# First FFN of a hybrid decoder layer: where a pair's products for the 16 learned tokens stand among the products of its up quad

## The chip, the cores and the metric

One core of a Trainium2 chip runs the whole layer. The metric is the time of one execution on the device, in microseconds (us). The engines of the core work side by side, each through its own queue in order: TensorE (PE in the profile, its weight loads PEld) multiplies matrices into PSUM banks, VectorE (DVE) and ScalarE (ACT) work element by element, GpSimd (POOL) mostly issues stores, SyncE (SP) issues most loads. They meet at semaphores.

## What is computed

16 learned ("meta") tokens stand ahead of 1024 tokens of 1024 values each, 1040 in all. The layer is a half-step gated FFN, a projection with two kinds of heads, an output projection and a second half-step FFN, each on normed tokens:

```python
def swiglu(h, w_in, w_out):
    gu = h @ w_in
    g, u = jnp.split(gu, 2, axis=-1)
    return (jax.nn.silu(g) * u) @ w_out

h = h + 0.5 * swiglu(rms_norm(h, ffn1_norm[l]), ffn1_w_in[l], ffn1_w_out[l])
```

All in float32. The case is about the first line of `swiglu` in the first FFN: 1024 input values, 2 x 2816 columns (gate g and up u), for the 1024 tokens and for the 16 learned ones.

## The kernel before

**Tiles.** `fast_in` (from L351) makes the first FFN's `h @ w_in` for the 1024 tokens. It takes 256 columns of gate and the same 256 of up at a time, a *pair*; there are 11 pairs. The gate half and the up half of a pair are each a *quad*: a 2 x 2 block product (two halves of the 1024 inputs, two blocks of 128 columns, two halves of 512 tokens) done with seven block products instead of eight (Winograd's scheme). The token side has seven ready operands, named B11, T2, B21, T3, T1, T4, B22 in the order in which a quad uses them; the weight side has seven to match: a11, s2, a12, s3, s1, a22, s4.

**Weights of a quad.** `block` (L367) loads four blocks of 128 x 512 float32 (256 KB each) from SP into buffers of tag raw, of which there are 10; the order is a11, a21, a22, a12. DVE makes the sums s1 = a21 + a22, s2 = s1 - a11, s3 = a11 - a21, s4 = a12 - s2 (L382, tag s, three buffers). `operand` (L358) splits each of the seven into a rounded part (ACT, L360) and a rest (DVE, L362), three buffers each, so that the split of an operand starts when the product three places ahead of it has ended. A product is 12 matmuls of 128 x 512 (L450).

**What happens to a product.** B11 and B21 go to bank qa, T2, T3 and T4 to qb, T1 and B22 to qc; a bank that takes several products in turn is read between them. After B11 ACT copies qa (p1). After T2 DVE reads qb (u2, L482), after T3 again (u3). After T1 DVE reads qc (L533 in a gate quad, u at L543 in an up quad), then after T4 qb, then after B22 qc. So T3 may not start before u2 has read qb, nor B22 before u has read qc; one other product stands between each time. In a gate quad ACT takes silu of the results; in an up quad DVE multiplies by them, and POOL stores.

**Learned tokens.** Their products can't use the block scheme; `begin` (L988), which `fast_in` calls as `meta(col, blocks)`, makes them from the same raw blocks. When it is called for a gate quad, it only keeps the four blocks, so their buffers stay in use. When it is called for the up quad, it first calls `finish` for the pair before (a transpose mf on PE at L978, silu sgm on ACT at L981, actm on DVE at L982), then issues 64 small matmuls (mq, L1001) that read all eight raw blocks of the pair, those of the first input half first, and a copy mt on ACT (L1010). sgm, mt and actm are placed after the last instruction of ACT and of DVE that belongs to a main product ("marks").

**Order.** PE's order is the order of the program text (`manual_schedule` for PE). The order of DVE, ACT, SP and POOL is laid out when the kernel is built, by a planner with a model of times: of what it takes to be ready, the earliest in the program's text first. The first eight quads (four pairs, "opened") run interleaved, in turns; the other seven pairs run one quad after the other (L609 to L612). Between the main work, single steps of other work are put in: splitting later weights ahead of time (L180, L181, stores L175), and transposing tokens (L1046).

**After it.** `fast_out` (L615) multiplies by `w_out` (L732, bank o). Its first buffers for `w_out` blocks (L634) and activations (L639) lie where B11 and B21, the first operands to be read for the last time, lay before.

The generator that hands out a quad's weight operands, one for each `next`, is this:

```python
            if not opened:
                yield operand(a11)
...
            yield operand(s3 if sums else made(a11, on.tensor_sub, a21, turns))
            if meta:
                meta(col, [(q, b) for q, b in zip(quarters, blocks)])
            yield operand(s1)
```

What stands between two `yield`s is issued when the next operand is asked for, which `go` (L459) does right ahead of its matmuls. So the learned tokens' group stands on PE between the quad's fourth product (T3) and its fifth (T1).

Of the kernel before, what the change touches and what calls it, by code (L numbers as in the profile page):

```python
# [48 lines left out]
class Block:  # L49
# [300 lines left out]
    def fast_in(self, ops, n, w_in, actD, openers, ev0, open_ev, feed=None, meta=None, spare=None,  # L350
# [7 lines left out]
        def operand(src):  # L358
            hi = wp.tile([P, 4, P], F32R, tag="wh", name="wh", bufs=3)
            nc.scalar.copy(hi, src)  # L360
            lo = wp.tile([P, 4, P], F32R, tag="wl", name="wl", bufs=3)
            self.block_lo = nc.vector.tensor_sub(lo, src, hi.bitcast(F32))  # L362
            return hi, lo
# [3 lines left out]
        def block(i, h, col):  # L367
            t = wp.tile([P, 4, P], F32, tag="raw", name="raw", bufs=self.in_bufs)
            with self.tc.issue_after(loaded[-1].ins) if loaded else ExitStack():
                loaded.append(nc.sync.dma_start(  # L370
                    t, w_in[512 * h : 512 * h + 512, col + P * i : col + P * i + P]
                    .rearrange("(k p) f -> p k f", p=P)
                ))
            self.block_load = loaded[-1]
            return t

        def made(x, op, y, turns):
            if turns == 2:
                t = self.early_raw.tile([P, 4, P], F32, tag="raw", name="s", bufs=4)
            else:  # L380
                t = wp.tile([P, 4, P], F32, tag="s", name="s", bufs=3)
            taken(op(t, x, y), False)  # L382
            return t
# [3 lines left out]
        def parted(src):  # L387
            places[0] += 1
            tags = ("wh", "wl") if places[0] % 2 else ("raw", "raw")
            got = []  # L390
            for i, tag in enumerate(tags):
                t = wp.tile([P, 4, P], F32R, tag=tag, name="w" + "hl"[i],
                            bufs=self.in_bufs if tag == "raw" else 3)
                nc.sync.dma_start(t.bitcast(F32).rearrange("p k f -> p (k f)"), src[:, i])
                got.append(t)
            return got

        prepared = {}
        quarters = (0, 0), (1, 0), (1, 1), (0, 1)
# [3 lines left out]
        def first_sums(blocks, turns, on):  # L403
            a11, a21, a22, _ = blocks
            s1 = made(a21, on.tensor_add, a22, turns)
            return s1, made(s1, on.tensor_sub, a11, turns)
# [11 lines left out]
        def weights(col, opened, turns):  # L418
            if opened and feed:
                for i, src in enumerate(self.parted2[col]):  # L420
                    first = self.first_w.pop(0) if self.first_w and i == 0 else None
                    yield first or parted(src)
                return
            if opened:
                for h in range(2):
                    yield operand(block(0, h, col))
            blocks, sums = prepared.pop(col, (None, None))
            blocks = blocks or [block(i, h, col) for i, h in quarters]
            a11, a21, a22, a12 = blocks
            if not opened:  # L430
                yield operand(a11)
            if sums:
                s1, s2, s3, s4 = sums
            else:
                s1, s2 = first_sums(blocks, turns, on)
            yield operand(s2)
            if not opened:
                yield operand(a12)
            yield operand(s3 if sums else made(a11, on.tensor_sub, a21, turns))
            if meta:  # L440
                meta(col, [(q, b) for q, b in zip(quarters, blocks)])
            yield operand(s1)
            yield operand(a22)
            yield operand(s4 if sums else made(a12, on.tensor_sub, s2, turns))
# [9 lines left out]

        def quad(col, take, opened=None, turns=0, keep=None):
            w = weights(col, opened, turns)
            ps, ready = {}, []

# [133 lines left out]
        opened = [q for f in range(0, 2 * openers, 2) for q in pair(f, "first")]  # L592
# [1799 lines left out]
```

## Time and profile before

| | us |
|---|---|
| median of 3 runs | 1959.63 (1957.4 to 1960.16) |
| profiled execution | 1959.65 |
| its span in the trace | 1957.9 |
| first and last start of an mq matmul | 79.2 and 461.1 |
| mt copies on ACT (L1010): count, median of one | 11, 0.266 |

The span is the time from the first to the last instruction that the profile holds; the execution's own time has 1.7 us around it. All times "at" something are counted from the start of the span. PE's granted clock was 1.00 in every stretch that is shown. A row of a view of stretches has, after start:end, the length, the busy time of PE, PEld, DVE, ACT and POOL, each with its count of instructions, then the granted clock, the share that the DMA engines were busy, and GB/s. A row of a wait view has who waited, for whom, the total in us, how many times, and the longest. A row of a timeline has start, duration, engine, line, operation, tiles, and in brackets the idle time ahead of it with what ended it.

### The profile page before, as it was taken

How to read it: one execution, taken by the hardware profiler on the slowest of the kernel's cores; microseconds unless marked ns; L12 is line 12 of the kernel's file. 1: busy time of each engine (PE TensorE's matmuls, PEld its weight loads, DVE VectorE, ACT ScalarE, POOL GpSimd, SP SyncE). 2: the span in 40 equal slices, each digit the busy share in tenths (PEclk: the TensorE clock that was granted, in tenths of full speed). 3: DMA queues.
4: the chain of work that ended last, by engine and by line, in shares of the span. 5: the costliest groups of instructions: out<-in, count | busy, mean ns of one | idle time of the engine just before them, and what ended most of it. 6: DMA issues, size and time to landing. Idle time of an engine off the chain costs nothing.

```text
span 1957.9 us, 30218 instructions
## 1 busy us (share of the span) xinstructions
PE 1919.8 (98%) x10607; PEld 1616.6 (83%) x10607; DVE 1390.4 (71%) x2184; ACT 849.6 (43%) x1711; POOL 450.5 (23%) x625
## 2 busy tenths in 40 slices
PE   7999999999999999999999999999999999999999
PEld 6888888788888888888898978887888888888887
DVE  7977877877678665467777766677567767766774
ACT  6523443334444544356666635433232332344443
POOL 3010100001000003133333332210544645530000
PEclk9999999999999999999999999999999999999999
DMA  7356887758965315865454177655634444469473
GB/s 213 93 165 170 253 272 243 233 203 291 375 221 188 127 54 144 193 170 148 128 148 121 57 253 225 161 208 183 198 115 140 128 131 121 132 243 318 154 231 113
DMA packets 381687, 355.54 MB, mean 182 GB/s; under 512 B 129040, under 2 KB 284560, under 8 KB 381536
## 3 DMA queue, kind: packets, MB, share of 16 engines
q1 hardware_dynamic: 359728, 288.98, 48.7%
q0 software_dynamic: 20768, 64.63, 9.5%
q8 instruction: 84, 1.38, 0.3%
q14 instruction: 67, 0.55, 0.1%
q10 hardware_dynamic: 1040, 0.00, 0.0%
HBM read 237.95 MB, written 115.57 MB: 181 GB/s over the span
## 4 chain that ended last, share of the span: by engine, by line
PE 89%; DVE 4%; DMA 3%; ACT 2%; issue 1%; POOL 1%; SPq 1%; DVEq 0%; ACTq 0%; POOLq 0%
PE o L732 21%; PE qb L450 18%; PE qa L450 12%; PE qc L450 12%; PE proj L249 5%; PE proj L251 4%; PE proj L250 4%; PE flip L1495 2%; PE wo L250 1%; PE wo L249 1%; PE wo L251 1%; PE mq L1001 1%; PE oacc L1572 1%; PE oacc L1570 1%; DMA oT<-oD 1%
## 5 line engine op out<-in xcount | busy, mean ns | idle before, releaser
L450 PE MATMUL qb<-T,wh 128*128 128x512 f32 x1056 | 344.6, 390 | 1.3 <-ACT T L309 0.8
L450 PEld LDWEIGHTS qb<-T,wh 128*128 128x128 f32 x1056 | 198.1, 188 | 46.4 <-issue 2.5
L450 PE MATMUL qa<-B,wh 128*128 128x512 f32 x696 | 226.7, 390 | 0.3 <-ACT B L835 0.2
L249 PE MATMUL proj<-xh,wh 128*128 128x512 f32 (+2 forms) x640 | 213.2, 333 | 2.6 <-ACT st L1142 1.3
L732 PE MATMUL o<-t,w 128*128 128x512 f32 x924 | 211.8, 390 | 0.7 <-DVE u L543 0.7
L251 PE MATMUL proj<-xl,wh 128*128 128x512 f32 (+2 forms) x640 | 210.2, 328 | 0.8 <-DVE xl L1957 0.8
L250 PE MATMUL proj<-xh,wl 128*128 128x512 f32 (+2 forms) x640 | 210.1, 328 | 0.0
L732 PE MATMUL o<-parts 128*128 128x512 f32 x924 | 209.6, 389 | 0.0
L450 PE MATMUL qb<-T,wl 128*128 128x512 f32 x528 | 205.5, 389 | 0.0
L732 PEld LDWEIGHTS o<-t,w 128*128 128x128 f32 x924 | 172.8, 188 | 37.8 <-ACT sgm L981 1.1
L732 PEld LDWEIGHTS o<-parts 128*128 128x128 f32 x924 | 173.5, 188 | 36.0
L362 DVE TENSOR_TENSOR wl<-s,wh 128x512 fp32r<-128x512 f32 x160 | 165.6, 1035 | 50.8 <-ACT wh L360 49.9
L360 ACT CAST wh<-s 128x512 fp32r<-128x512 f32 x160 | 99.2, 622 | 188.5 <-PE qb L450 141.1
L450 PEld LDWEIGHTS qa<-B,wh 128*128 128x128 f32 x696 | 130.5, 188 | 28.0 <-DVE B L836 0.5
L360 ACT CAST wh<-raw 128x512 fp32r<-128x512 f32 x120 | 74.4, 621 | 155.8 <-PE qc L450 111.4
L450 PE MATMUL qa<-B,wl 128*128 128x512 f32 x348 | 135.4, 389 | 0.0
L249 PEld LDWEIGHTS proj<-xh,wh 128*128 128x128 f32 x640 | 120.8, 189 | 15.0 <-ACT st L1142 2.2
L251 PEld LDWEIGHTS proj<-xl,wh 128*128 128x128 f32 x640 | 120.7, 189 | 12.3 <-DVE xl L1957 1.2
L250 PEld LDWEIGHTS proj<-xh,wl 128*128 128x128 f32 x640 | 120.8, 189 | 10.1
L450 PE MATMUL qc<-B,wh 128*128 128x512 f32 x352 | 115.1, 390 | 2.3 <-DVE u L543 2.3
L450 PE MATMUL qc<-T,wh 128*128 128x512 f32 x352 | 117.0, 394 | 0.0
L450 PEld LDWEIGHTS qb<-T,wl 128*128 128x128 f32 x528 | 99.1, 188 | 20.2
(393 smaller groups left out, 3819.4 us busy)
## 6 DMA issues: line engine op xcount, KB each, us to landing
raw<-in_ffn_w_in_dram SPq DMA_DIRECT2D x176, 256.0 KB, 4.0
raw<-in_ffn_w_out_dram SPq DMA_DIRECT2D x112, 256.0 KB, 4.5
w2in<-both SPq DMA_DIRECT2D x28, 512.0 KB, 3.4
raw<-in_w_in_dram SPq DMA_DIRECT2D x25, 512.0 KB, 5.2
ks<-kD SPq DMA_DIRECT2D x32, 260.0 KB, 4.8
wout<-both SPq DMA_DIRECT2D x16, 512.0 KB, 3.7
wh<-w2in SPq DMA_DIRECT2D x27, 256.0 KB, 3.1
wl<-w2in SPq DMA_DIRECT2D x27, 256.0 KB, 3.1
```

The costliest lines, as they stand in the source:

```text
L249: nc.tensor.matmul(ps, wh[:, s], xs, start=k == 0, stop=False)
L250: nc.tensor.matmul(ps, wl[:, s], xs, start=False, stop=False)
L251: nc.tensor.matmul(ps, wh[:, s], xl[:, k, c0 : c0 + n], start=False, stop=k == nk - 1)
L360: nc.scalar.copy(hi, src)
L362: self.block_lo = nc.vector.tensor_sub(lo, src, hi.bitcast(F32))
L450: nc.tensor.matmul(ps, a[:, k, :], b[:, k, :], start=start and k == 0 and i == 0, stop=k == 3 and i == 2, skip_group_check=True,)
L732: nc.tensor.matmul(banks[bank][m], y[:, m * P : (m + 1) * P], z, start=start and at == 0 and e == 0, stop=q == nq - 1 and e == 2, skip_gro ...
L1001: nc.tensor.matmul(ps[at : at + 32, :], self.xm[:, 4 * h + k, :], got[i, h][:, k, :], start=h == 0 and k == 0, stop=h == 1 and k == 3, til ...
L1495: self.nc.tensor.transpose(ps[:m, j, :], src[:, s0 : s0 + m], self.ident)
L1570: nc.tensor.matmul(o[:, c], vj, w[0], start=j == 0, stop=False, skip_group_check=True)
L1572: nc.tensor.matmul(o[:64, c], vj[:, :64], w[1], start=False, stop=end, skip_group_check=True)
```

## The change

In a quad of one of the seven pairs that are not opened, `meta` is now called ahead of the first operand, right after the four blocks' loads are issued; in an opened pair it stays where it was. For a gate quad the call only keeps the blocks. For an up quad the group (mf of the pair before, mq, and the work on ACT and DVE that hangs on them) now stands on PE ahead of the quad's first product, B11, instead of between T3 and T1.

```diff
             a11, a21, a22, a12 = blocks
+            if meta and not opened:
+                meta(col, [(q, b) for q, b in zip(quarters, blocks)])
             if not opened:
                 yield operand(a11)
             if sums:
...
             yield operand(s3 if sums else made(a11, on.tensor_sub, a21, turns))
-            if meta:
+            if meta and opened:
                 meta(col, [(q, b) for q, b in zip(quarters, blocks)])
             yield operand(s1)
```

The second FFN calls `fast_in` without `meta`; nothing changes there.

## The prediction

> **What bounds the kernel now.** I read the engine table first, then the busy time of the first FFN in stretches cut at the start of each pair's T1 product, and then the waits of TensorE (PE) in these stretches.
>
> ```profile
> PE 1919.8 (98%) x10607; PEld 1616.6 (83%) x10607; DVE 1390.4 (71%) x2184; ACT 849.6 (43%) x1711; POOL 450.5 (23%) x625
> ...
> 256.66:297.01 40.35, 40.35 (x234) 33.28 (x234) 31.63 (x51) 16.60 (x30) 3.79 (x7) 1.00 0.91 279
> 297.01:337.35 40.34, 40.34 (x235) 33.22 (x234) 32.60 (x53) 15.93 (x29) 3.80 (x7) 1.00 0.77 241
> 337.35:379.40 42.05, 40.58 (x234) 33.21 (x234) 32.61 (x53) 16.04 (x29) 3.79 (x7) 1.00 0.69 222
> 379.40:420.40 41.00, 40.69 (x234) 33.27 (x235) 32.02 (x52) 15.83 (x29) 3.79 (x7) 1.00 0.61 209
> 420.40:461.35 40.95, 40.48 (x234) 33.09 (x234) 32.02 (x52) 16.04 (x29) 3.79 (x7) 1.00 0.63 220
> ...
> PE qc L450 <- DVE u L543: 2.3, 3, 1.5
> ```
>
> PE is busy 98% of the span, so the change can win only what PE idles in this stage. A pair without a stall takes 40.35 us. The three stretches from 337.35 on take 42.05, 41.00 and 40.95: 1.70 + 0.65 + 0.60 = **2.95 us** too much. The wait row names 2.3 of it: three times the B22 product (bank qc) waits until DVE has read that bank (u, L543).
>
> Why DVE is late there is in the chain that ended last, first a pair with a stall, then the loads of the next two, then a pair without one (start, duration, what).
>
> ```profile
> 335.34 0.11 PE mf L978
> 335.45 1.02 PE mq L1001 x32
> 336.47 5.15 DMA raw<-in_ffn_w_in_dram
> ...
> 341.71 0.70 DVE s L382
> 342.42 0.02 issue
> 342.44 1.29 DVE s L382 x2
> 343.73 0.61 DVE u L543
> 344.35 0.14 issue
> 344.48 1.63 PE qc L450 x6
> ...
> 378.52 3.98 DMA raw<-in_ffn_w_in_dram
> ...
> 419.43 4.21 DMA raw<-in_ffn_w_in_dram
> ...
> 254.77 1.88 PE mq L1001 x64
> 256.66 2.95 PE qc L450 x12
> 259.61 2.49 PE qb L450 x11
> ...
> 284.13 2.72 PE qa L450 x12
> ```
>
> Half of the learned tokens' group (mq, 32 of 64 matmuls, 1.02 us) has to pass before blocks of this pair's gate are free. Only then SP loads the next gate's remaining blocks there (5.15 us). DVE, which works in order, stands at the sum a21 + a22 of that next gate (L382) until a22 lands, and behind it waits u, for which PE waits. The DVE's waits say how regular this is (six pairs from 216.35 on), and its timeline gives two of the waits that did not reach PE:
>
> ```profile
> DVE s L382 <- DMA raw<-in_ffn_w_in_dram: 22.7, 6, 4.8
> ...
> 300.27 0.69 DVE L382 TENSOR_TENSOR s<-raw 128x512 f32<-128x512 f32 x1 [3.73 <-DMA raw<-in_ffn_w_in_dram]
> ...
> 341.71 0.69 DVE L382 TENSOR_TENSOR s<-raw 128x512 f32<-128x512 f32 x1 [4.83 <-DMA raw<-in_ffn_w_in_dram]
> ```
>
> DVE stands still in every pair; PE feels it only where load and sums together outlast PE's work up to B22.
>
> **The change part by part.** *What moves.* In the 7 pairs after the four opened ones, mf (0.11 us), mq (1.88) and what hangs on them (ACT's sgm and mt copy, DVE's actm) go from between T3 and T1 to ahead of B11, four products of 2.72 = 10.9 us earlier. No instruction is added or removed, so PE's work stays: 0. The product after the group takes 2.95 instead of 2.72; that 0.23 passes from T1 to B11: 0.
>
> *The wait removed.* Count from the start of mq. Before: 1.88 + 2.95 + 2.72 (T1, T4), so B22 could start at 7.55; in the pair above the bank was free at 344.48 − 335.45 = 9.03, 1.48 late. Afterwards the first product to need a bank that DVE has just read is the up quad's T3 (it adds to T2's bank, which u2 reads first). It comes after B11 (2.95), T2 and B21 (2.72 each): 1.88 + 8.39 = 10.27. Even if the whole old chain, load, three sums and a read of the bank, stood ahead of it, it would be through at 9.03, **1.24 us to spare**, and this was the worst of the pairs. It should not even stand there:
>
> ```profile
> 246.50 2.72 PE qb L450 x12
> ...
> 248.19 0.69 DVE L362 TENSOR_TENSOR wl<-s,wh 128x512 fp32r<-128x512 f32 x1 [1.10 <-ACT wh L360]
> 248.92 0.69 DVE L382 TENSOR_TENSOR s<-raw,s 128x512 f32<-128x512 f32 x1
> ```
>
> The sums of a quad have three buffers (tag s), and the up quad's fourth sum (248.92) takes the one that s3's split (248.19) leaves. The next gate's first sum finds a buffer only after that. The fourth sum comes 248.92 − 246.50 = 2.42 after T2's start; with T2 at 1.88 + 2.95 = 4.83 from mq, that is 7.25, later than the load's 1.02 + 5.15 = 6.17. So the block should be there before DVE asks, and of the 22.7 us little should be left. What is late next is nothing: around T1 to B22 only the usual splits remain. I take the full −2.95; bounds 0 (the wait moves along) and −2.95.
>
> The Trainium skill, "DMA: Bandwidth & Descriptors", "Anatomy of one DMA", prices a transfer at about 2.0 us plus bytes over 436 KB/us (fitted on another issue path), which would be an estimate of 2.6 us for these 256 KB. The rows say 3.98 to 5.15. By the page's price old B22 would never have waited for a load and the change would bring 0.
>
> *The wait added.* PE now needs all eight blocks of the pair before B11, and everything on PE queues behind mq.
>
> ```profile
> 255.79 4.01 SPq L370 DMA_DIRECT2D raw<-in_ffn_w_in_dram  x6
> ...
> DMA to landing us min/median/max: 4.0/4.8/7.0
> ```
>
> Six loads, the up quad's four last among them, are out by 259.80 and down by 266.8 even at the longest 7.0; that up quad begins at 284.13. 17 us of cover, and earlier release only widens it: 0. If it went, each us late would be a us of PE, seven times.
>
> *Slack that shrinks.* T1, T4 and B22 lose the 2 us that the group gave their operands. Those are split three products ahead, as buffers come free; 0, bounds 0 to +0.5. On ACT, mt and sgm now stand behind the gate's last silu; ACT is 43% busy and nobody waits for them before the next pair: 0.
>
> *The end of the stage.* In the last pair the token operands B11 and B21 are read for the last time, and so freed, 1.99 us later against the end of the stage (1.88 + 0.11), and w_out's first loads go to that place.
>
> ```profile
> 452.16 0.38 SPq L634 DMA_DIRECT2D raw<-in_ffn_w_out_dram  x1
> 456.44 0.32 SPq L639 DMA_DIRECT2D act<-act10B  x1
> 456.80 0.43 SPq L634 DMA_DIRECT2D raw<-in_ffn_w_out_dram  x1
> 458.94 0.32 SPq L175 DMA_DIRECT2D w2in<-both  x1
> 459.36 0.40 SPq L639 DMA_DIRECT2D act<-act11B  x1
> 459.82 0.90 SPq L634 DMA_DIRECT2D raw<-in_ffn_w_out_dram  x1
> ...
> PE o L732 <- DVE u L543: 0.7, 1, 0.7
> ```
>
> The first load and the 456.44/456.80 pair move by 2; the third load, whose split stands in DVE's queue ahead of the last u, goes back to back behind them and moves from 459.82 to about 460.3. So the 0.7 us that PE waits there grows by about 0.4. Bounds: −0.7 and +2.0. I take +0.4, nearest to the SP rows.
>
> **Sum:** −2.95 + 0.4 = −2.55. The profiled execution took 1959.65 us (span 1957.9 and 1.7 around it), the median of the runs is 1959.63: 1959.65 − 2.55 = **1957.1 us**.
>
> **The rivals.**
>
> *A. The wait moves along.* The planner puts DVE's and SP's queues in order; it can put the next gate's loads behind a store that waits on SP, or its sum elsewhere ahead of a bank read, and DVE stalls as before. For: its order already trusted loads that came 3.7 to 4.8 us late. Against: the buffer count and 1.24 us of spare. 1959.6 us; chance 0.13.
>
> *B. Slower: DVE blocks the up quad's T3.* The same DVE wait, now ahead of u2 in all seven pairs. It decides at 10.27 us after mq's start. With the longest landing, 1.02 + 7.0, three sums (2.02), u2 (0.61) and issue (0.14) make 10.79: 0.52 late, and with one more split of 0.60 queued between, 1.12. Seven times 1.12 is 7.8; less the 2.95 saved, +4.9: 1964.5 us. Over 0.98 per pair the kernel is slower by over 0.2%. Against: the median landing is 4.8. Chance 0.12.
> The Trainium skill ("DMA: Bandwidth & Descriptors", "Latency and other measured facts") lets HBM access grow from 0.2 us to 2 us under load, so loads moved into a fuller stretch would land up to 1.8 us later, an estimate: 9.03 + 1.8 = 10.83, this rival without the extra split (1960.6). The trace does not bear it out: DVE waited 3.73 us at a DMA share of 0.91 and 4.83 at 0.69.
>
> *C. The end of the stage takes it back.* The ring's 2 us go fully to PE: 1959.65 − 2.95 + 2.0 = 1958.7; chance 0.13. Against: the third load's place above.
>
> *D. Faster: the new order helps later stages.* Only PE's order is written out by hand; the rest is planned anew behind the change.
>
> ```profile
> PE flip L1495 <- DVE wu L1619: 3.6, 9, 0.8
> ...
> PE z L1640 <- ACT sig L1643: 1.9, 5, 0.5
> PE flip L1495 <- DVE wm L1619: 1.8, 3, 0.6
> ```
>
> Of these 7.3 us, half gone would give 1953.5. It can as well add; nothing in the rows says which. Chance 0.14.
>
> **How the numbers follow.** Forecast 0.48. A measurement of this kernel tells about 0.2% (3.9 us) from no change, so faster means under 1955.7 and slower over 1963.5. Forecast, A and C lie within: 0.74, of which 0.02 goes to faster for a forecast that also loses the 0.7 at the stage's end and a little more. Faster 0.16, same 0.72, slower 0.12. The range 1954.5 to 1961.5 leaves out B at its price and half of D, about 0.19; it holds A, C and B's small form.
>
> **What would show it.** Right: pair stretches of 40.35 us throughout; no PE wait for u at qc; DVE's 22.7 us at L382 nearly gone; SP rows of the next gate's loads about 11 us earlier against B22; the mt copy right behind a silu. Wrong: a PE wait at qb (T3) for u2, or at mq for a DMA; more than 1.2 us at the first o product; PE waits of the later stages that differ by more than 1 us in sum.

## The result, and the profile after

| | median, us (lowest to highest) | runs | ratio to before (95% interval) |
|---|---|---|---|
| before | 1959.13 (1956.74 to 1962.09) | 21 | |
| changed | 1961.88 (1960.06 to 1964.73) | 21 | 1.0014 (1.0008 to 1.0020) |

The change makes the kernel 2.75 us **slower**, where 2.55 us faster was forecast. The time lies just above the range's end of 1961.5.

The stage that the change was about did what was forecast. This is the view of stretches of the changed kernel, cut again at the start of each pair's T1 (length, busy PE, PEld, DVE, ACT, POOL, granted clock, DMA share, GB/s):

```profile
256.76:297.06 40.30, 40.30 (x234) 33.28 (x234) 32.25 (x51) 16.24 (x30) 3.77 (x7) 1.00 0.90 281
297.06:337.37 40.31, 40.31 (x235) 33.29 (x234) 33.07 (x53) 15.81 (x29) 3.80 (x8) 1.00 0.79 247
337.37:377.68 40.31, 40.31 (x235) 33.29 (x234) 33.06 (x53) 15.81 (x29) 3.78 (x7) 1.00 0.75 238
377.68:417.99 40.31, 40.31 (x234) 33.29 (x234) 32.45 (x52) 15.81 (x29) 3.78 (x7) 1.00 0.61 205
417.99:458.30 40.31, 40.31 (x234) 33.29 (x234) 31.23 (x50) 15.81 (x29) 3.78 (x7) 1.00 0.50 184
```

Every pair takes 40.31 us and PE is never idle: the 42.05, 41.00 and 40.95 are gone. DVE's order in the second of these pairs shows why:

```profile
291.32 0.69 DVE L382 TENSOR_TENSOR s<-raw,s 128x512 f32<-128x512 f32 x1
293.62 0.69 DVE L382 TENSOR_TENSOR s<-raw 128x512 f32<-128x512 f32 x1
294.35 0.69 DVE L382 TENSOR_TENSOR s<-s,raw 128x512 f32<-128x512 f32 x1
```

The next gate's first sum (293.62) comes behind the up quad's fourth (291.32), as the three s buffers demand, and it carries no wait for a load. Of the 22.7 us that DVE waited there before, nothing is left. DVE now waits for ACT's halves of the splits instead (29.5 us in these six pairs, 10.6 before), and PE waits for neither.

The loss is what follows, the hand-over to `fast_out`. PE's timeline from the stage's last transpose (mf) to the first products of learned tokens (m), before:

```profile
469.58 0.27 PE L978 MATMUL mf<-ident,mt 128*128 128x128 f32 x1
470.59 19.32 PE L732 MATMUL o<-t,w 128*128 128x512 f32 x84 [0.73 <-DVE u L543]
489.84 1.74 PE L1969 MATMUL m<-raw,actm 128*32 128x128 f32 x56
```

and after (line numbers are 2 higher; the last row is of the view of stretches):

```profile
466.30 0.27 PE L980 MATMUL mf<-ident,mt 128*128 128x128 f32 x1
467.76 8.63 PE L734 MATMUL o<-t,w 128*128 128x512 f32 x37 [1.19 <-DVE u L545]
476.74 3.18 PE L734 MATMUL o<-t,w 128*128 128x512 f32 x11 [0.35 <-DVE w L651]
483.40 0.50 PE L734 MATMUL o<-t,w 128*128 128x512 f32 x1 [3.48 <-ACT w L650]
484.13 9.82 PE L734 MATMUL o<-t,w 128*128 128x512 f32 x35 [0.22 <-DVE w L651]
493.88 1.74 PE L1971 MATMUL m<-raw,actm 128*32 128x128 f32 x56
...
484.00:488.00 4.00, 3.87 (x10) 3.08 (x11) 3.68 (x7) 1.43 (x3) 0.00 (x0) 0.59 0.96 349
```

mf comes 3.28 us earlier: the gain. From mf to m the same 84 products take 27.58 us instead of 20.26: **7.32 us** lost. Of these, 4.51 are waits (1.19 + 0.35 + 3.48 + 0.22 = 5.24, 0.73 before). Behind the longest wait the granted clock falls (0.59 over 484 to 488, last row): 0.41 of 4 us, about 1.6 us of work not done. The rest, 1.2 us, lies in the short rows beside the gaps (11 products take 3.18 us where the 84 of before take 0.23 each, a lone one 0.50); what makes these slow is not shown.

The long wait names ACT. Its timeline and SP's show what ACT stood at. ACT after:

```profile
471.71 0.62 ACT L650 CAST t<-act 128x512 fp32r<-128x512 f32 x1 [1.65 <-PE o L734]
472.62 0.62 ACT L650 CAST t<-act 128x512 fp32r<-128x512 f32 x1 [0.28 <-PE o L734]
482.21 0.62 ACT L650 CAST t<-act 128x512 fp32r<-128x512 f32 x1 [8.97 <-DMA act<-act16B]
482.74 1.66 ACT L650 CAST w<-raw 128x512 fp32r<-128x512 f32 x3
```

SP after:

```profile
463.57 0.32 SPq L641 DMA_DIRECT2D act<-act15B  x1
467.04 0.32 SPq L175 DMA_DIRECT2D w2in<-both  x1
467.46 1.43 SPq L2062 DMA_DIRECT2D hT<-xD  x2
470.04 1.52 SPq L175 DMA_DIRECT2D w2in<-both  x2
471.62 1.15 SPq L2062 DMA_DIRECT2D hT<-xD  x1
472.81 1.33 SPq L636 DMA_DIRECT2D raw<-in_ffn_w_out_dram  x1
474.24 0.80 SPq L641 DMA_DIRECT2D act<-act16B  x1
```

and SP before:

```profile
465.06 0.90 SPq L634 DMA_DIRECT2D raw<-in_ffn_w_out_dram  x2
467.46 0.33 SPq L639 DMA_DIRECT2D act<-act15B  x1
468.06 0.33 SPq L639 DMA_DIRECT2D act<-act16B  x1
468.67 0.32 SPq L639 DMA_DIRECT2D act<-act17B  x1
469.87 0.32 SPq L175 DMA_DIRECT2D w2in<-both  x1
```

The planner has laid out SP's queue anew. The seventh w_out block (raw) and the seventh activation (act16B) stood ahead of the last three stores of split weights (w2in) and of the loads of hT between them; now they stand behind them. The stores wait for DVE's splits, so act16B is issued at 474.24, 7.94 us after mf, where before it was 1.52 us ahead of mf. It takes until 482 to land (7.9 us from its issue, 3.4 before). ACT has the casts of three activations ahead of those of three w_out blocks, so these blocks wait at ACT behind act16B, and PE behind them.

The two profiled executions differ by 0.4 us only (1960.06 and 1959.65), because the one of before lost time later that the other did not: a stretch at a lower clock and waits for loads. Both views are of the kernel before:

```profile
860.00:866.00 6.00, 4.74 (x20) 3.01 (x18) 4.45 (x8) 5.21 (x14) 1.18 (x3) 1.00 0.49 146
866.00:872.00 6.00, 5.91 (x21) 4.68 (x22) 5.39 (x8) 2.74 (x9) 3.54 (x5) 0.72 0.95 207
...
PE wo L251 <- DMA oT<-oD: 1.5, 1, 1.5
PE wo L250 <- DMA wl<-wout: 0.8, 1, 0.8
```

The changed kernel waited 0.7 at the first of these and not at the second. The medians, 2.75 apart, are what is to be explained: about 3 gained, about 6 lost.

### The profile page after: what moved, and what is told of

It reads as the page before. It is cut to its first block, busy times and chain, and to the rows that moved or that the text cites. A ratio compares the mean times of both kernels' runs of the same rounds, so it can differ in the third digit from the quotient of the medians.

```text
span 1958.3 us, 30199 instructions
## 1 busy us (share of the span) xinstructions
PE 1920.0 (98%) x10607; PEld 1616.7 (83%) x10607; DVE 1393.5 (71%) x2184; ACT 847.4 (43%) x1711; POOL 449.8 (23%) x625
## 4 chain that ended last, share of the span: by engine, by line
PE 88%; DVE 4%; DMA 3%; ACT 2%; issue 1%; SPq 1%; POOL 1%; DVEq 0%; ACTq 0%; POOLq 0%
PE o L734 21%; PE qb L452 18%; PE qa L452 12%; PE qc L452 12%; PE proj L249 5%; PE proj L251 4%; PE proj L250 4%; PE flip L1497 2%; PE wo L250 1%; PE wo L251 1%; PE wo L249 1%; PE mq L1003 1%; PE oacc L1574 1%; PE oacc L1572 1%; DMA wl<-wout 1%
```

## The experiments

Differences are medians against the kernel before on the same chip.

**1. The last pair left alone; the last pair alone.** In place of `not opened`, the group goes ahead of B11 where this holds (the first kernel has `!=`, the second `==`):

```diff
-            if meta and not opened:
+            ahead = meta and not opened and col % D_FF != D_FF - 2 * P
+            if ahead:
                 meta(col, [(q, b) for q, b in zip(quarters, blocks)])
...
-            if meta and opened:
+            if meta and not ahead:
```

> The group stands ahead of B11 in six pairs; in the last pair it stays between T3 and T1, as before. Theory (the six pairs bring about 3 us, since DVE no longer waits for the next gate's blocks; the loss sits in the hand-over to fast_out and comes from the last pair alone): 1956 us, 3 under before; the first o product waits 0.7 us as before and no o product waits for ACT. Rival 1 (the loss comes with the loads of all pairs being earlier, or with the planner's new order as a whole): the hand-over loses 5 to 7 us as in the changed kernel, 1961 to 1962. Rival 2 (the later stages eat the gain, because what they wait for is loads with a clock of their own): about 1959.

Measured: 1955.26 against 1958.18, −2.92 us, ratio 0.9985 (0.9977 to 0.9994).

> The group stands ahead of B11 in the last pair alone; the other ten pairs are as before. Theory: the three stalls of 2.3 us at B22 are there again and the hand-over loses as in the changed kernel: before plus 5 to 6 us, 1964 to 1965, with an o product that waits about 3.5 us for ACT. Rival 1 (the hand-over's loss needs the earlier pairs' move): 1959. Rival 2 (the 2 us later release of B11 and B21 is the whole price): 1961.

Measured: 1964.50 against 1958.18, +6.32 us, ratio 1.0032 (1.0021 to 1.0044). PE waits of the stage and the hand-over, first with the last pair left alone, then with the last pair alone:

```profile
PE o L735 <- DVE u L546: 0.7, 1, 0.7
PE qb L453 <- DVE u L485: 0.2, 1, 0.2
...
PE o L735 <- ACT w L651: 3.3, 1, 3.3
PE qc L453 <- DVE u L546: 2.8, 3, 1.2
PE o L735 <- DVE u L546: 1.6, 1, 1.6
```

The two parts come apart. Six pairs bring about 3 us (in this profile mf comes 1.87 us earlier) and cost nothing at the hand-over; the last pair, which has no next gate to load for, brings nothing and costs about 6. Their sum, +3.4, lies within the change's interval (1.0008 to 1.0020, 1.6 to 3.9 us). The rivals that put the loss into earlier loads, or into the stage as a whole, fall.

**2. Half of the group.** The 32 matmuls of the gate's blocks go ahead, the 32 of the up blocks stay behind T3 (core of the edit; a bank is opened by the first call):

```diff
-            if meta and not opened:
-                meta(col, [(q, b) for q, b in zip(quarters, blocks)])
+            if meta and not opened:
+                meta.ahead(col)
...
+            if now:
+                products(banks[col], [(0, dict(gates.pop(col - D_FF)))])
```

> In the seven pairs only the half of the group that reads the gate's blocks (32 matmuls) and the transpose of the pair before go ahead of B11; the half that reads the up blocks stays between T3 and T1. Theory for the gain (the gate's buffers come free earlier; it doesn't matter where the up half stands): the pairs take 40.3 us throughout and no B22 product waits. Rival: the up half holds buffers too, and a part of the three stalls stays. Theory for the loss (in SP's queue, act of the seventh q stands behind three stores of split weights): here this load stands behind them again while the seventh w_out block does not, so if the activation is what ACT waits for, the o product waits 3 us or more and the time is 1961 to 1962; if it is the w_out block, the loss goes and the time is 1956 to 1957.

Measured: 1974.23 against 1958.18, +16.05 us, ratio 1.0086 (1.0072 to 1.0100). No B22 waits any more, so the gate's buffers alone were what the loads waited for. The hand-over loses with act16B behind the stores though the w_out block is ahead of them (PE waits 2.2 us for ACT, ACT 6.63 for act16B, last two rows below): the activation suffices. But the time is 12 us over what was expected, for a reason that no theory had. One pair's two halves in PE's timeline, and the two rows of the hand-over:

```profile
288.91 1.94 PE L996 MATMUL mq<-raw,xm 128*32 128x128 f32 x32
301.89 1.94 PE L996 MATMUL mq<-raw,xm 128*32 128x128 f32 x32
...
PE o L734 <- ACT w L650: 2.2, 1, 2.2
...
494.76 0.62 ACT L650 CAST t<-act 128x512 fp32r<-128x512 f32 x1 [6.63 <-DMA act<-act16B]
```

32 matmuls take 1.94 us; the undivided 64 took 1.96. The four groups of 32 columns run side by side, and a half uses two of them at a time for just as long. Twice 1.94 less 1.96 is 1.92 us more for each pair, 13.4 in seven. Less the 3 gained, and with 4.55 lost at the hand-over (24.81 us from mf to m), that makes 15 of the 16.05 measured. In the trace the pairs take 42.4 us from one mf to the next, 2.1 more than 40.3, which is the better part of the rest.

**3. The sum moved instead of the group.** Before, with only the next gate's first two sums placed behind u:

```diff
-                    nc.vector.tensor_add(u, ps, plus)
+                    added = nc.vector.tensor_add(u, ps, plus)
+                    if (i, j) == (1, 1):
+                        read[:] = [added.ins]
...
-                s1, s2 = first_sums(blocks, turns, on)
+                at = meta and not opened and col < D_FF and read
+                with self.tc.issue_after(read[0]) if at else ExitStack():
+                    s1, s2 = first_sums(blocks, turns, on)
```

> The kernel before, with the group where it was; only the next gate's first two sums on DVE are placed behind the reading of bank qc after T1 (u). The loads come as late as before. Theory (PE's three stalls come from DVE standing at that sum ahead of u): no B22 product waits, the pairs take 40.35 us throughout, DVE still waits for the loads but a few us less, the hand-over is as before: 1956 us, 3 under before. Rival (DVE is short of time between T1 and B22, or the late loads make the next gate's operands late): the stalls stay or move to the next gate's T2: 1959 or more.

Measured: 1954.88 against 1958.18, −3.30 us, ratio 0.9984 (0.9976 to 0.9993). DVE's largest wait in total over the seven pairs now reads:

```profile
DVE u L545 <- PE qc L452: 23.5, 7, 3.5
```

DVE stands for PE to finish T1, instead of PE for DVE; PE waits nowhere in these pairs. Here the loads are as late as before (the next gate's six start 1.3 us after mf in both kernels), so it was not their lateness but DVE's standing for them ahead of u that cost PE the three stalls. The expectation missed one point: no wait of DVE for the loads is left at all.

**4. The hand-over: SP's order and ACT's order.** Three kernels. In the changed kernel, the last three stores go to POOL:

```diff
+        left = sum(len(makes) for _, makes in groups)
...
-                nc.sync.dma_start(split[0], split[1].bitcast(F32))
+                left -= 1
+                (nc.gpsimd if left < 3 else nc.sync).dma_start(split[0], split[1].bitcast(F32))
```

> The changed kernel, with the last three stores of split weights (w2in) issued by POOL instead of SP. In SP's queue the seventh w_out block and the seventh activation then stand behind three loads of hT, but behind no store that waits for DVE. Theory (these two loads come late because SP, in order, stands at the stores): the seventh activation is issued before 470 us instead of at 474.2, no o product waits for ACT over 1 us, and the time is that of the kernel with the last pair left alone, 1955 to 1956. Rival (the 2 us later release of B11 and B21, or the full DMA engines, make the loads late whatever the queue's order): an o product waits 2 us or more still, 1959 to 1962.

Measured: 1957.82 against 1958.08, −0.26 us, ratio 0.9998 (0.9989 to 1.0007). SP's row of the load and ACT's of its cast:

```profile
469.13 0.79 SPq L643 DMA_DIRECT2D act<-act16B  x1
...
479.58 0.62 ACT L652 CAST t<-act 128x512 fp32r<-128x512 f32 x1 [6.07 <-DMA act<-act16B]
```

It lies between the two. act16B is issued 2.1 us after mf instead of 7.9, but is there only 10 us later, and PE still waits 1.6 us. Of the 6 lost, about 3 are back. So the three stores are a part of it; for the rest the load is late though they no longer stand ahead of it on SP. Full DMA engines alone don't explain that: their share is 0.99 from 468 to 480 in this kernel, but 1.00 in the kernel before, where the same load landed in 3.4 us. There it was issued ahead of the stores and of the loads of hT; here three of those loads are still ahead of it, and the stores go out beside it. Which of these makes it late was not tried.

In the changed kernel, ACT's casts are put in the order w, t for each q from 4 on (`rounded[0]` is the w cast just ahead):

```diff
+                    at = self.apart and a == "A12" and q > 3
+                    with self.tc.issue_after(rounded[0]) if at else ExitStack():
+                        xh, xl = halved(act, "t", n)
```

> The changed kernel, with the casts on ACT at the start of fast_out in the order w, t for each q from 4 on, instead of the t of q 4, 5, 6 and then the w of q 4, 5, 6. SP's queue is the same there, so the seventh activation is as late as in the changed kernel. Theory (PE waits because ACT, in order, stands at the cast of that one activation while w blocks that have landed wait behind it): the products of q 4 and 5 come ahead of the wait, 5.4 us of cover; the wait of 3.5 us falls under 1 us, the clock stays full there, 1956 to 1957. Rival (the other blocks are late too): 1960 or more, with a wait for w or t of q 4 or 5.

Measured: 1955.56 against 1958.08, −2.52 us, ratio 0.9990 (0.9981 to 0.9999). act16B is issued as late as in the changed kernel, and PE does not feel it:

```profile
474.50 0.47 SPq L641 DMA_DIRECT2D act<-act16B  x1
...
468.05 19.73 PE L737 MATMUL o<-t,w 128*128 128x512 f32 x84 [0.76 <-DVE u L545]
```

84 products in one run of 19.73 us. So what turns a late load into 6 us is ACT's order: one cast that waits, ahead of three others. (The block of the third of these was issued at 472.81 and took 8.0 us, so it came little earlier than act16B; the first two could run.)

Last, the kernel before with SP's order alone (core of the edit; `last_store` is the last store of split weights):

```diff
+                    at = self.apart and a == "A12" and q == 6
+                    with self.tc.issue_after(self.last_store.ins) if at else ExitStack():
                         src, blocks = left(a, q)
                         act = right((q, b), n)
```

> The kernel before, its group in the old place in all pairs; only the loads of the seventh w_out block and the seventh activation are placed behind the last store of split weights in SP's queue, which is the order that the changed kernel has. B11 and B21 come free as early as before. Theory (that order alone makes the hand-over slow): an o product waits about 3 us for ACT, 26 to 27 us from the last transpose mf to the first m product instead of 20.3, and the time is before plus 5 to 6 us, 1963 to 1964. Rival (the later release of B11 and B21, 2 us, is part of the loss): before plus 2 to 4 us, 1960 to 1962.

Measured: 1963.16 against 1957.80, +5.36 us, ratio 1.0025 (1.0014 to 1.0035). PE's timeline, and two stretches of it:

```profile
470.79 0.27 PE L980 MATMUL mf<-ident,mt 128*128 128x128 f32 x1
471.80 11.16 PE L734 MATMUL o<-t,w 128*128 128x512 f32 x48 [0.74 <-DVE u L543]
485.51 11.57 PE L734 MATMUL o<-t,w 128*128 128x512 f32 x36 [2.55 <-ACT w L648]
497.02 1.74 PE L1971 MATMUL m<-raw,actm 128*32 128x128 f32 x56
...
485.00:488.00 3.00, 2.49 (x5) 1.76 (x6) 2.51 (x5) 2.61 (x5) 0.00 (x0) 0.50 1.02 371
488.00:492.00 4.00, 4.00 (x11) 3.08 (x11) 2.24 (x4) 1.12 (x3) 0.00 (x0) 0.52 1.01 362
```

26.23 us from mf to m with the group in its old place and B11 and B21 freed as early as ever: 5.97 of the 7.32 lost. The order alone makes most of the loss, and the later release isn't needed for it. (The time's interval, 2.7 to 6.9 us, would also allow the upper end of the rival's 2 to 4; and in the profiled execution the pairs stalled 1.2 us more than before, with mf at 470.79 instead of 469.58.)

From mf to m in the profiled executions, beside the medians:

| kernel | mf to m, us | median less before, us |
|---|---|---|
| before | 20.26 | |
| changed | 27.58 | +2.75 |
| last pair left alone | 20.25 | −2.92 |
| last pair alone | 27.50 | +6.32 |
| half of the group | 24.81 | +16.05 |
| before, sum behind u | 20.59 | −3.30 |
| changed, stores on POOL | 22.65 | −0.26 |
| changed, w casts first | 20.68 | −2.52 |
| before, SP's order alone | 26.23 | +5.36 |

Three kernels beat both: the six pairs without the last, the sum behind u, and, by a little less, the changed kernel with the w casts first.

## Why the prediction was wrong, step by step

*The wait removed, −2.95.* Right in mechanism and size: −2.92 with the last pair left alone, −3.28 at mf in the profile (−1.87 in the profile with the last pair left alone). The buffer argument held too, and the next gate's loads came 8 to 11 us earlier: in the pair whose T1 starts at 337.4 in both kernels, the first at 325.40 and the other five from 328.29, where before all six start from 336.47. The sum moved alone shows that a smaller edit does the same.

*No instruction added, the wait for all eight blocks, shrinking slack, mt and sgm later on ACT.* Right: pairs of 40.31 us, no wait at mq, at T1 or at T3. Rivals A and B did not come about. One reading in B is off: the DMA share of 0.91 set beside DVE's wait of 3.73 us is that of the stretch before it. During the two waits the share was about the same (0.95 from 296.15 to 300.27, 0.93 from 336.47 to 341.71), so they say little about a load's time in a fuller stretch.

*The end of the stage, +0.4, bounds −0.7 and +2.0.* This step failed. It measured about +6 (7.32 in the profile). It took the rows of SP's queue of before, moved them by the 2 us of the later release, and let what stood behind go "back to back", in the same order. But SP's order is laid out by the planner, and with the group moved in the last pair it changed: the seventh w_out block and the seventh activation went behind three stores. The upper bound had the same fault, since it held a shift of 2 us at most; rival C, at +2.0, named the place and missed the size. Rival A had the mechanism, a load put behind a store that waits on SP, but for the next gate's loads. And the step followed SP only as far as the third load and the first o product. There the wait did grow as it was priced (0.73 to 1.19 us), but by luck: the third load was issued 7.55 us ahead of mf instead of 9.76, so 2.2 later and not 0.5, and with the w casts first it is 7.55 ahead as well, where that wait is 0.76. Who waits behind the seventh on ACT, which was in the trace as three t casts ahead of three w casts, was not asked.

*Rival D* had a new order of the plan in it, but for the later stages. The waits there (flip, z) hardly changed: 3.6, 1.9 and 1.8 became 3.5, 1.4 and 1.8.

What stays open is why the planner's model puts the two loads behind the stores when the group stands ahead in the last pair. DVE's split of the third w_out block comes later in its queue there, behind those of two activations (464.45 us), and the kernel's text places the load of the seventh block behind that split (`issue_after(los[-4])`, in both kernels). The later release of B11 could make that split late; but only the effect of the order was tried, not its cause.

## What to carry to other kernels

In a kernel whose queues are planned, a moved group can change the order of queues that it does not touch, here at the seam where its buffers go to the next stage: compare there the order of each queue, not only the times. A term for such a seam needs the bound of a re-ordered queue (one late load, with what waits behind it in order on each engine), not that of a shift. And where an effect comes from one member of a loop and the cost from another, the last turn can be left out: here that is 2.9 us faster instead of 2.75 slower.

## What the runs showed of the hardware that was not expected

**A gap of PE can cost more than itself.** After PE idled 3.48 us in the changed kernel the clock was 0.59 over 4 us, 1.6 us of work; after 2.55 us with SP's order alone it was at half for almost 7 (0.50 and 0.52 over 7 us), which is 3.4 us of work, more than the gap; after 1.63 us with the stores on POOL it stayed at 1.00. The Trainium skill, "TensorE: Matmul & The Clock Gate", "Part 1: The HAM clock gate", has the clock fall to half after an idle window of about 3.4 us. The first case agrees with it; the second fell after a shorter gap, and the kernel before fell to 0.72 in a stretch (866 to 872) in which PE was busy for 5.91 of 6.00 us, without any long gap ahead of it: the 6 us before have 4.74 of PE in short pieces, with no gap over 0.5 us.

**Half of a packed group takes as long as the whole:** 1.94 us for 32 matmuls on two column groups, 1.96 for 64 on four. The Trainium skill, "TensorEngine Tiling (Array Packing)", "Key Properties", says that tiles work in parallel and independently; the rows agree.
